# Splitting each 1 MB weight unit with one copy and one subtraction of 2048 columns

## The chip, the cores and the metric

The kernel runs on one core of a Trainium2 chip. The metric is the time of one execution in device microseconds (us); lower is better. One execution of the kernel before was also taken by the hardware profiler, and every row below is from that execution.

## The reference

Two transformer-like blocks, one after the other, on 256 tokens of width 2048, all in float32. Cut to the matrix products and what hangs between them:

```python
# first block
h = rms_norm(x, norm_mix_pre)
qa, ka, va, qn, kn, vn, gates = split(h @ w_in)
oa = rms_norm(diff_attention(rope(qa), rope(ka), va, lam), subln_w)
on = neighbourhood_attention(qn, kn, vn, na_rpb)
g_a, g_b = split(sigmoid(gates))
y = (g_a * (oa @ w_branch_a) + g_b * (on @ w_branch_b)) @ w_out
x = x + rms_norm(y, norm_mix_post)
u = square(relu(rms_norm(x, norm_mlp_pre) @ w_up))
x = x + rms_norm(u @ w_down, norm_mlp_post)
# second block
proj = rmsnorm(x, norm_w) @ w_in2          # mLSTM and HGRN2 inputs, gates ml_i, ml_f
y = concat(mlstm(...), hgrn2(...))
h = x + y @ w_out2
gate = sigmoid(rmsnorm(h, pe_norm_w) @ w_pg)
out = rmsnorm(h + gate * (p @ w_pe), final_norm_w)
```

The weights are float32 and each is used once, for 256 tokens.

## The kernel before, in words

**Numbers.** A float32 product is made of three products in the format fp32r: the weight is split into a high part `wh` (the weight rounded by a copy) and a low part `wl` (the weight less `wh`); the activation likewise into hi and lo. TensorE then adds hi·wh, hi·wl and lo·wh in PSUM.

**Weight units.** The weights come in units of 1 MB, a raw tile of 128 x 2048 float32 (8 KB in each partition; pool `raw`, three buffers), each by one DMA on SP's queue (`load_unit`). `split_w` splits a unit in two halves of 1024 columns: ScalarE (ACT) copies raw to `wh` (L100), VectorE (DVE) subtracts `wh` from raw to give `wl` (L101). The tiles of `wh` and `wl` are half a unit each, 4 KB in a partition, and the pool `wsplit` has four buffers of each, so two units' worth. A copy into a buffer waits until the last matmul that read the buffer's old half is done. There are 334 full units, so 668 copies and 668 subtractions; the first matrix, w_0, is split by lines of its own in the startup loop (L327, L328).

**Who uses a unit.** `panel` (L115 to L147) makes a 256 x 512 result from several units, 24 matmuls of 128x512 a unit (L128 hi·wh, L129 hi·wl, L130 lo·wh), for the two token tiles t=0 and t=1 in turn. For the last `lead` units it does all of t=0 first and then t=1, so that what follows for t=0 begins early; lead is 2 for the last panel of w_out, of w_down and of w_pg, and 1 elsewhere. `chunk_mm` (L149 to L173) makes a transposed 128-column result from one unit: 8 wide matmuls on `wh` (L156), 16 narrow ones on `wl` (L161), 8 wide. `chunk_pair` (L187, L192) does the first two units of w_up together, k-tile by k-tile, while their input is still being transposed. `embed` (L555 to L557) multiplies p by the two units of w_pe, between the end of a panel and the transposes of the residual.

**What sets the order.** Nothing is ordered by hand apart from a few priorities: a scheduler of the framework puts each engine's instructions into a list, and each engine runs its own list strictly in that order. An instruction that waits holds back everything behind it on its engine. Weight copies and subtractions stand in the same lists as all the other work of ACT and DVE.

**Places that the steps touch.** The q and k chunks with their rotary embedding (L358 to L361 after `halves`, L200 and L201), which also wait for a transfer of small columns, `cols`; the attention (L422 to L445); the post-norms after w_out and w_down (`yw` L607, sums L271 and L564, updates of the residual `res` L577, transposes L257, their splits L247 and L248, `embed`); the gate of the mLSTM (`log_f`, transposed sums L836, gate L837); the final panels of w_pg with their sigmoid (L979) and the closing norm (`finish`, L991 to L1006).

Of the kernel before, what the change touches and what calls it, by code (L numbers as in the profile page):

```python
# [9 lines left out]
F32 = mybir.dt.float32  # L10
F32R = mybir.dt.float32r
I8 = mybir.dt.int8
I32 = mybir.dt.int32
AF = mybir.ActivationFunctionType
ALU = mybir.AluOpType
AX = mybir.AxisListType

P = 128
# [39 lines left out]
def body(nc, tc, a, tap=lambda n, x: None):  # L58
    with ExitStack() as ctx:
        _body(ctx, nc, tc, a, tap)  # L60


def _body(ctx, nc, tc, a, tap):
    V, S, G, TE = nc.vector, nc.scalar, nc.gpsimd, nc.tensor

    def pool(name, bufs=1, psum=False, stack=ctx):
        kw = {"space": bass.MemoryType.PSUM} if psum else {}
        return stack.enter_context(tc.tile_pool(name=name, bufs=bufs, **kw))

    cpool = pool("const")  # L70
    rawp = pool("raw", 3)
    wp = pool("wsplit", 4)
    actp = pool("act", 16)
    mmp = pool("mm", 4, True)
    tpp = pool("tp", 2, True)
# [4 lines left out]
    def nm(s):  # L80
        uid[0] += 1
        return f"{s}_{uid[0]}"
# [10 lines left out]
    def act2():  # L93
        return actp.tile([P, 2, 2, T], F32R, tag="act", name=nm("act"))


    def split_w(r):
        wh = wp.tile([P, 1024], F32R, tag="wh", name=nm("wh"))
        wl = wp.tile([P, 1024], F32R, tag="wl", name=nm("wl"))
        S.activation(wh, r, AF.Copy)  # L100
        V.tensor_tensor(wl, r, wh.bitcast(F32), ALU.subtract)  # L101
        return wh, wl

    def load_unit(src):
        raw = rawp.tile([P, 2048], F32, tag="raw", name=nm("raw"))
        nc.sync.dma_start(raw, src)
        parts = []
        for h in range(2):
            parts.append(split_w(raw[:, h * 1024 : (h + 1) * 1024]))
        return parts  # L110

    pending = []

# [4 lines left out]
    def panel(src, acts, nunits, lead=1):  # L118


        ps = [ps_mm(), ps_mm()]
        nk = nunits * 4

        def step(t, kt, parts):
            k = kt % 4
            wh, wl = (w[:, (k % 2) * 512 : (k % 2 + 1) * 512] for w in parts[k // 2])
            h, l = acts.hi(kt, t), acts.lo(kt, t)
            TE.matmul(ps[t], h, wh, start=(kt == 0), stop=False)  # L128
            TE.matmul(ps[t], h, wl, start=False, stop=False)  # L129
            TE.matmul(ps[t], l, wh, start=False, stop=(kt == nk - 1))  # L130

        last = []
        for u in range(nunits):
            parts = load_unit(src[u])
            if u >= nunits - lead:
                last.append((u, parts))
                continue
            for kt in range(4 * u, 4 * u + 4):
                for t in range(2):
                    step(t, kt, parts)  # L140
            if u == 0:
                flush()
        for t in range(2):
            for u, parts in last:
                for kt in range(4 * u, 4 * u + 4):
                    step(t, kt, parts)
        return ps  # L147
# [23 lines left out]
    def chunk(src, acts):  # L171
        parts = load_unit(src)
        ps = ps_mm()  # L173
        chunk_mm(ps, parts, acts, 16)
        flush()
        return ps

    def chunk_pair(src_a, src_b, acts):

        parts = [load_unit(src_a), load_unit(src_b)]  # L180
        ps = [ps_mm(), ps_mm()]
        for kt in range(16):
            w = [[p[kt // 8][s][:, (kt % 8) * P : (kt % 8 + 1) * P] for s in range(2)] for p in parts]

            def wide():
                for i in range(2):
                    TE.matmul(ps[i], w[i][0], acts.both(kt), start=(kt == 0), stop=(kt == 15))  # L187

            if kt < 15:
                wide()  # L190
            for i in range(2):
                TE.matmul(ps[i][:, 0:T], w[i][1], acts.hi(kt), start=False, stop=False)  # L192
            if kt == 15:
                wide()
        return ps
# [90 lines left out]
    def later(tile_, src, after):  # L286

        G.tensor_copy(tile_[0:1, 0:1], after)
        nc.gpsimd.dma_start(tile_, src)
# [24 lines left out]
    for g in range(8):  # L314
        xn.tiles.append(act2())
        raw = raws[g // 2][:, g % 2 * 1024 : (g % 2 + 1) * 1024]
        wh = wp.tile([P, 1024], F32R, tag="wh", name=nm("wh"))
        wl = wp.tile([P, 1024], F32R, tag="wl", name=nm("wl"))
        n = 2 if g == 0 else 1
        for j in range(2):  # L320
            kt = 2 * g + j
            c, h, x = cols0[:, kt : kt + 1], xn.hi(kt), xts[g // 2][:, kt % 4, :]
            S.activation(h, x, AF.Copy, scale=c)
            V.scalar_tensor_tensor(xn.lo(kt), x, c, h.bitcast(F32), ALU.mult, ALU.subtract)
            if j < n:
                sl = slice(j * 1024 // n, (j + 1) * 1024 // n)
                S.activation(wh[:, sl], raw[:, sl], AF.Copy)  # L327
                V.tensor_tensor(wl[:, sl], raw[:, sl], wh[:, sl].bitcast(F32), ALU.subtract)  # L328

        def mm(j, c, part):  # L330
            kt = 2 * g + j
            sl = slice((4 * j + c) * P, (4 * j + c + 1) * P)
            if part == 0:
                TE.matmul(first[c], wh[:, sl], xn.both(kt), start=(kt == 0), stop=(kt == 15))
            else:
                TE.matmul(first[c][:, 0:T], wl[:, sl], xn.hi(kt), start=False, stop=False)

        if g < 7:
            for j in range(2):
                for part in range(2):  # L340
                    for c in range(4):
                        mm(j, c, part)
        else:
            for c in range(4):
                for j, part in ((0, 0), (0, 1), (1, 1), (1, 0)):
                    mm(j, c, part)
        if g == 1:
            there = xn.hi(2 * g)[0:1, 0:1].bitcast(F32)
            cstA = tA.tile([P, NCONST_A], F32, name="cstA")
            later(cstA, a["constsA"], there)  # L350
# [154 lines left out]
    for c in range(32):  # L505
        g = gates[c // 4][:, c % 4, :]
# [7 lines left out]
    for c in range(16):  # L514
        parts = load_unit(a["w_br"][c])
        ps = [ps_mm(), ps_mm()]
        for b, acts in enumerate((oa, on)):
            g = gates[4 * b + c // 4][:, c % 4, :]
# [91 lines left out]
    parts = load_unit(a["w_pe"][0])  # L610
# [38 lines left out]
    parts = load_unit(a["w_pe"][1])  # L649
# [476 lines left out]
```

## Time and profile before

| | us |
|---|---|
| three runs | 2010.0, 2006.1, 2008.21 |
| their median | 2008.21 |
| the profiled execution, whole | 2008.86 |
| its span in the profile | 2006.7 |
| PE (TensorE matmuls) busy | 1983.7, 99% |
| DVE busy, ACT busy | 1221.2 (61%), 1019.4 (51%) |
| POOL (GpSimd) busy | 156.5 (8%) |
| DMA, mean rate over the span | 185 GB/s |

The span is the time from the first to the last instruction of the profiled execution; the 2.2 us between it and the whole lie around it. PE is TensorE's matmuls, PEld its weight loads, which overlap them. The profile's granted clock is a share of TensorE's full speed; over the span its mean is 0.996. A row of a timeline gives start, duration, engine, line, operation, tiles and, in brackets, how long the engine had been idle before and what ended that. Matmul ends are modelled in such a profile, so the distance from one start to the next is the better measure of a matmul.

### The profile page before, as it was taken

What the parts mean: (1) busy time and instruction counts of PE and PEld (TensorE: products, weight loads), DVE (VectorE), ACT (ScalarE), POOL (GpSimd) and SP (SyncE); (2) the same over time, 40 slices, a digit from 0 to 9 for tenths busy, and PEclk for the clock granted to TensorE, in tenths of its full rate; (3) what the DMA queues carried; (4) which work ended last, traced back from release to release, by engine and by line L of the source; (5) the groups of instructions that cost most, each with busy time, mean ns of one, the idle gap of its engine ahead of it and who ended that gap; (6) DMA issues with size and microseconds to landing.
All of it is one profiled execution on the core that took longest, in us unless ns stands there. A gap on an engine that the chain in (4) does not pass through costs nothing. (4 is left out here: it accounts for less than half of the span.)

```text
span 2006.7 us, 25627 instructions
## 1 busy us (share of the span) xinstructions
PE 1983.7 (99%) x10192; PEld 1684.4 (84%) x10192; DVE 1221.2 (61%) x1574; ACT 1019.4 (51%) x1491; POOL 156.5 (8%) x190
## 2 busy tenths in 40 slices
PE   9999999999999999999999999999999999999997
PEld 7888888888888888888888888887788877888886
DVE  6756546555765765466556556656567864565565
ACT  6756446544554654455345434445543445444465
POOL 1400102111220000000000000010001110000011
PEclk9999999999999999999999999999999999999999
DMA  7753554455566455555555555555553344555553
GB/s 263 245 199 118 189 189 162 163 189 189 185 234 223 175 202 189 191 188 190 197 195 190 192 189 189 189 193 175 193 175 140 106 168 141 185 191 198 187 189 126
DMA packets 54375, 370.74 MB, mean 185 GB/s; under 512 B 6112, under 2 KB 6400, under 8 KB 10736
## 3 DMA queue, kind: packets, MB, share of 16 engines
q1 hardware_dynamic: 52208, 360.21, 51.0%
q0 software_dynamic: 1760, 8.38, 1.1%
q8 instruction: 80, 1.31, 0.3%
q10 hardware_dynamic: 288, 0.52, 0.1%
q14 instruction: 39, 0.32, 0.0%
HBM read 366.99 MB, written 2.10 MB: 184 GB/s over the span
## 5 line engine op out<-in xcount | busy, mean ns | idle before, releaser
L101 DVE TENSOR_TENSOR wl<-raw,wh 128x1024 fp32r<-128x1024 f32 x668 | 838.5, 1257 | 450.9 <-ACT wh L100 441.6
L100 ACT ACTIVATE wh<-raw 128x1024 fp32r<-128x1024 f32 x668 | 705.6, 1057 | 430.1 <-PE mm L130 365.1
L156 PE MATMUL mm<-act,wh 128*128 128x512 f32 x2592 | 634.5, 393 | 0.0
L156 PEld LDWEIGHTS mm<-act,wh 128*128 128x128 f32 x2592 | 473.4, 188 | 89.2
L128 PE MATMUL mm<-wh,act 128*128 128x512 f32 x1344 | 525.6, 391 | 0.8 <-ACT act L247 0.8
L129 PE MATMUL mm<-wl,act 128*128 128x512 f32 x1344 | 524.8, 390 | 0.4 <-DVE wl L101 0.4
L130 PE MATMUL mm<-wh,act 128*128 128x512 f32 x1344 | 524.4, 390 | 0.0
L161 PEld LDWEIGHTS mm<-act,wl 128*128 128x128 f32 x2592 | 335.8, 191 | 15.5 <-DVE wl L101 1.5
L161 PE MATMUL mm<-act,wl 128*128 128x256 f32 x2592 | 343.7, 283 | 1.1 <-DVE wl L101 1.1
L128 PEld LDWEIGHTS mm<-wh,act 128*128 128x128 f32 x1344 | 253.0, 188 | 53.6 <-ACT act L247 1.2
L129 PEld LDWEIGHTS mm<-wl,act 128*128 128x128 f32 x1344 | 253.0, 188 | 53.5 <-DVE wl L101 1.2
L130 PEld LDWEIGHTS mm<-wh,act 128*128 128x128 f32 x1344 | 252.9, 188 | 52.9 <-issue 0.6
L200 ACT ACTIVATE z<-mm 128x256 f32<-128x256 f32 x159 | 60.8, 383 | 280.4 <-PE mm L156 277.0
L201 DVE TENSOR_TENSOR zu<-mm,z 128x256 f32<-128x256 f32 x64 | 27.1, 425 | 110.5 <-ACT z L200 110.4
L648 POOL TENSOR_TENSOR yw<-yw,wrow 128x512 f32<-128x512 f32 x6 | 7.8, 1307 | 686.7 <-ACT junk L271 686.7
L201 DVE TENSOR_TENSOR g<-mm,z 128x256 f32<-128x256 f32 x48 | 20.2, 424 | 63.8 <-ACT z L200 63.8
L200 ACT ACTIVATE zl<-mm 128x256 f32<-128x256 f32 x24 | 9.1, 379 | 62.8 <-PE mm L156 62.8
L508 POOL TENSOR_TENSOR g<-g,r1row 128x256 f32<-128x256 f32 x32 | 23.7, 741 | 146.4 <-DVE g L201 146.4
L271 ACT ACTIVATE junk<-res 128x512 f32<-128x512 f32 (+1 forms) x40 | 21.7, 543 | 18.7 <-DVE res L964 11.6
L247 ACT ACTIVATE act<-tp,cols 128x256 fp32r<-128x256 f32 x56 | 24.7, 477 | 11.2 <-DVE act L248 8.5
L732 PEld LDWEIGHTS at<-g,g 128*128 128x128 f32 x224 | 26.4, 191 | 3.0 <-issue 2.5
L522 POOL TENSOR_TENSOR g<-g,zm 128x256 f32<-128x256 f32 x32 | 23.7, 742 | 65.8 <-DVE zm L201 65.8
(300 smaller groups left out, 1051.8 us busy)
## 6 DMA issues: line engine op xcount, KB each, us to landing
raw<-in_w_q SPq DMA_DIRECT2D x84, 1024.0 KB, 4.8
raw<-in_w_up SPq DMA_DIRECT2D x64, 1024.0 KB, 4.8
raw<-in_w_down SPq DMA_DIRECT2D x64, 1024.0 KB, 4.8
raw<-in_w_in SPq DMA_DIRECT2D x40, 1024.0 KB, 4.8
raw<-in_w_out SPq DMA_DIRECT2D x32, 1024.0 KB, 4.8
raw<-in_w_v SPq DMA_DIRECT2D x16, 1024.0 KB, 4.8
raw<-in_w_br SPq DMA_DIRECT2D x16, 1024.0 KB, 4.8
raw<-in_w_pg SPq DMA_DIRECT2D x16, 1024.0 KB, 4.8
```

The costliest lines, as they stand in the source:

```text
L100: S.activation(wh, r, AF.Copy)
L101: V.tensor_tensor(wl, r, wh.bitcast(F32), ALU.subtract)
L128: TE.matmul(ps[t], h, wh, start=(kt == 0), stop=False)
L129: TE.matmul(ps[t], h, wl, start=False, stop=False)
L130: TE.matmul(ps[t], l, wh, start=False, stop=(kt == nk - 1))
L156: TE.matmul(ps, w, acts.both(kt), start=(kt == 0), stop=(kt == nk - 1))
L161: TE.matmul(ps[:, 0:T], w, acts.hi(kt), start=False, stop=False)
L200: S.activation(lo, ps[:, T : 2 * T], AF.Copy)
L201: V.tensor_tensor(out, ps[:, 0:T], lo, ALU.add)
L247: last = S.activation(h, src[:, i, :], AF.Copy, scale=colscale(kt + i))
L508: G.tensor_tensor(g, g, r1row, ALU.mult)
L732: TE.matmul(ps[:, h, :], kk[:, h, b0 : b0 + P], q[:, h, b0 : b0 + P], start=True, stop=True)
```

## The change

A unit is split by one copy and one subtraction of 2048 columns. The tiles of `wh` and `wl` are whole units of 8 KB in a partition, with two buffers of each in place of four halves: the same bytes, and the same two units' worth. The users get views of the two halves, so the matmuls are the same. The startup loop keeps its instructions and shares one whole tile between two of its eight steps.

```diff
-    wp = pool("wsplit", 4)
+    wp = pool("wsplit", 2)
...
-    def split_w(r):
-        wh = wp.tile([P, 1024], F32R, tag="wh", name=nm("wh"))
-        wl = wp.tile([P, 1024], F32R, tag="wl", name=nm("wl"))
-        S.activation(wh, r, AF.Copy)
-        V.tensor_tensor(wl, r, wh.bitcast(F32), ALU.subtract)
-        return wh, wl
+    def split_tiles():
+        return (wp.tile([P, 2048], F32R, tag=tag, name=nm(tag)) for tag in ("wh", "wl"))
 
     def load_unit(src):
         raw = rawp.tile([P, 2048], F32, tag="raw", name=nm("raw"))
         nc.sync.dma_start(raw, src)
-        parts = []
-        for h in range(2):
-            parts.append(split_w(raw[:, h * 1024 : (h + 1) * 1024]))
-        return parts
+        wh, wl = split_tiles()
+        S.activation(wh, raw, AF.Copy)
+        V.tensor_tensor(wl, raw, wh.bitcast(F32), ALU.subtract)
+        return [(wh[:, h * 1024 : (h + 1) * 1024], wl[:, h * 1024 : (h + 1) * 1024]) for h in range(2)]
...
-        wh = wp.tile([P, 1024], F32R, tag="wh", name=nm("wh"))
-        wl = wp.tile([P, 1024], F32R, tag="wl", name=nm("wl"))
+        if g % 2 == 0:
+            wh2, wl2 = split_tiles()
+        wh, wl = (w[:, g % 2 * 1024 : (g % 2 + 1) * 1024] for w in (wh2, wl2))
```

ACT and DVE have 334 instructions fewer each, PE and SP as many as before. Because the scheduler weighs the durations of all instructions, the lists change in other places too. Line numbers of the changed kernel are two or three lower than those of the kernel before, and the two instructions of the split stand at L105 and L106. In the rows that follow, a name's first number is the tile's, so two rows with one name touch one tile.

DVE after w_out's last panel, before: `yw0` and `yw1` take the panel's results of t=0 and t=1, the L577 updates add them to the residual, and `wl_1090` and `wl_1092` are halves of w_pe's first unit.

```order
L607 TENSOR_TENSOR yw0_5358<-mm_1056_5801,wrow_5357 128x512
L564 TENSOR_REDUCE s_1080_5944<-s_983_5368 128x1
L101 TENSOR_TENSOR wl_1090_5964<-raw_1088_5961,wh_1089_5963 128x1024
L226 RECIPROCAL s_1082_5948<-s_1081_5946 128x1
L577 SCALAR_TENSOR_TENSOR res0_5349<-yw0_5358,s_1082_5948,res0_5349 128x512 x4
L101 TENSOR_TENSOR wl_1092_5968<-raw_1088_5961,wh_1091_5967 128x1024
L607 TENSOR_TENSOR yw1_5359<-mm_1057_5802,wrow_5357 128x512
```

The same place after the change (`wl_866` is w_pe's first unit, whole):

```order
L605 TENSOR_TENSOR yw0_4982<-mm_840_5377,wrow_4981 128x512
L562 TENSOR_REDUCE s_856_5504<-s_791_4992 128x1
L106 TENSOR_TENSOR wl_866_5524<-raw_864_5521,wh_865_5523 128x2048
L605 TENSOR_TENSOR yw1_4983<-mm_841_5378,wrow_4981 128x512
L562 TENSOR_REDUCE s_861_5515<-s_791_4992 128x1
L223 RECIPROCAL s_858_5508<-s_857_5506 128x1
L575 SCALAR_TENSOR_TENSOR res0_4973<-yw0_4982,s_858_5508,res0_4973 128x512 x3
```

The whole low part of w_pe's unit, and `yw1` too, now stand ahead of the first update of the residual; before, only half of the low part did.

ACT where the pair of w_up units ends, before: L271 are sums for the next norm, `z_1140` and `z_1143` take the pair's two results, and `wh_1147` and `wh_1154` are halves of weight units that follow the pair.

```order
L100 ACTIVATE wh_1147_6225<-raw_1144_6219 128x1024
L271 ACTIVATE junk_1131_6188,s_1125_6177<-res1_5350 128x512
L271 ACTIVATE junk_1132_6190,s_1125_6177<-res0_5349 128x512
L271 ACTIVATE junk_1133_6192,s_1125_6177<-res1_5350 128x512
L200 ACTIVATE z_1140_6205<-mm_1123_6111 128x256
L200 ACTIVATE z_1143_6213<-mm_1124_6112 128x256
L224 ACTIVATE s_1135_6196<-s_1134_6194,eps_78 128x2
L100 ACTIVATE wh_1154_6272<-raw_1153_6270 128x1024
```

The same place after the change (`wh_915` is the unit of the chunk that follows the pair):

```order
L268 ACTIVATE junk_903_5740,s_895_5725<-res1_4974 128x512
L221 ACTIVATE s_905_5744<-s_904_5742,eps_78 128x2
L197 ACTIVATE z_910_5753<-mm_893_5659 128x256
L197 ACTIVATE z_913_5761<-mm_894_5660 128x256
L105 ACTIVATE wh_915_5769<-raw_914_5767 128x2048
```

No copy of the next unit stands ahead of the pair's results any more; the first one stands behind both of them.

PE in the last panel of w_pg, after the change: `mm_2193` collects t=0 and `mm_2194` t=1; `wh_2202` and `wl_2203` are the last unit but one, `wh_2205` and `wl_2206` the last.

```order
L127 MATMUL mm_2193_14917<-wh_2202_14981,act_2095_14327 128x512
L125 MATMUL mm_2193_14917<-wh_2205_14987,act_2111_14439 128x512
L125 MATMUL mm_2194_14918<-wh_2202_14981,act_2093_14317 128x512
L126 MATMUL mm_2194_14918<-wl_2203_14982,act_2093_14317 128x512
L127 MATMUL mm_2194_14918<-wh_2202_14981,act_2093_14317 128x512
L125 MATMUL mm_2194_14918<-wh_2202_14981,act_2093_14317 128x512
L126 MATMUL mm_2194_14918<-wl_2203_14982,act_2093_14317 128x512
L127 MATMUL mm_2194_14918<-wh_2202_14981,act_2093_14317 128x512
L125 MATMUL mm_2194_14918<-wh_2202_14981,act_2095_14327 128x512
L126 MATMUL mm_2193_14917<-wl_2206_14988,act_2111_14439 128x512
```

Before, the matmul on the last unit's low part came directly behind the first one on its high part; now seven matmuls of t=1 lie between them. The same seven lie there in the last panels of w_out and of w_down.

DVE at the gate of the mLSTM, before (`gate` is made from the transposed sums `tp`, the two L837 instructions are for t=0 and t=1):

```order
L793 SCALAR_TENSOR_TENSOR g4_2317_13205<-g4_2353_13422,cols_77,g4_2317_13205 128x256 x3
L101 TENSOR_TENSOR wl_2415_13760<-raw_2413_13757,wh_2414_13759 128x1024
L837 SCALAR_TENSOR_TENSOR gate_13643<-tp_2407_13711,s_2075_11783,cols_77 128x8 x2
L841 TENSOR_SCALAR s_2393_13664<-gate_13643 128x8
L101 TENSOR_TENSOR wl_2417_13764<-raw_2413_13757,wh_2416_13763 128x1024
```

and after the change:

```order
L791 SCALAR_TENSOR_TENSOR g4_1785_12149<-g4_1813_12350,cols_77,g4_1785_12149 128x256 x3
L835 SCALAR_TENSOR_TENSOR gate_12555<-tp_1857_12619,s_1591_10823,cols_77 128x8 x2
L839 TENSOR_SCALAR s_1845_12576<-gate_12555 128x8
L106 TENSOR_TENSOR wl_1863_12664<-raw_1861_12661,wh_1862_12663 128x2048
```

The subtraction that stood ahead of the gate stands behind it.

## Rows read from the trace of the kernel before

**Rows 1.** The page: busy time of each engine, and the two costliest groups.

```profile
PE 1983.7 (99%) x10192; PEld 1684.4 (84%) x10192; DVE 1221.2 (61%) x1574; ACT 1019.4 (51%) x1491; POOL 156.5 (8%) x190
...
L101 DVE TENSOR_TENSOR wl<-raw,wh 128x1024 fp32r<-128x1024 f32 x668 | 838.5, 1257 | 450.9 <-ACT wh L100 441.6
L100 ACT ACTIVATE wh<-raw 128x1024 fp32r<-128x1024 f32 x668 | 705.6, 1057 | 430.1 <-PE mm L130 365.1
```

**Rows 2.** PE's waits over the span: total us, times, longest us.

```profile
PE tp L267 <- POOL A L718: 2.0, 1, 2.0
PE tp L836 <- DVE gate L837: 1.8, 1, 1.8
...
PE mm L161 <- DVE wl L101: 1.1, 1, 1.1
```

**Rows 3.** Waits of SP's queue, the longest sum, same columns.

```profile
SPq L106 <- DVE wl L101: 1327.8, 239, 17.0
```

**Rows 4.** Groups by shape, startup: busy us, mean ns, idle us before.

```profile
L328 DVE TENSOR_TENSOR wl<-raw,wh 128x1024 fp32r<-128x1024 f32 x7 | 8.6, 1225 | 1.7 <-ACT wh L327 1.7
...
L327 ACT ACTIVATE wh<-raw 128x1024 fp32r<-128x1024 f32 x7 | 7.4, 1060 | 1.3 <-DVE act L324 0.5 <-DMA raw<-in_w 0.4
L328 DVE TENSOR_TENSOR wl<-raw,wh 128x512 fp32r<-128x512 f32 x2 | 1.4, 692 | 0.9 <-ACT wh L327 0.9
L327 ACT ACTIVATE wh<-raw 128x512 fp32r<-128x512 f32 x2 | 1.2, 622 | 0.9 <-DMA raw<-in_w 0.9
```

**Rows 5.** Timeline of ACT in a steady panel of w_down.

```profile
830.21 1.06 ACT L100 ACTIVATE wh<-raw 128x1024 fp32r<-128x1024 f32 x1 [1.66 <-PE mm L130]
832.93 1.06 ACT L100 ACTIVATE wh<-raw 128x1024 fp32r<-128x1024 f32 x1 [1.66 <-PE mm L130]
```

**Rows 6.** Timeline of ACT, then of DVE, in the first q chunks.

```profile
30.78 1.05 ACT L100 ACTIVATE wh<-raw 128x1024 fp32r<-128x1024 f32 x1
...
40.73 0.16 DVE L390 TENSOR_TENSOR s<-cols 128x2 f32<-128x2 f32 x1 [3.11 <-DMA cols<-in_cols]
```

**Rows 7.** Groups of DVE by shape, the attention, 145 to 200 us.

```profile
L101 DVE TENSOR_TENSOR wl<-raw,wh 128x1024 fp32r<-128x1024 f32 x14 | 17.1, 1224 | 8.8 <-ACT wh L100 6.0 <-issue 2.7
```

**Rows 8.** Timeline after w_out's last panel, DVE, then ACT.

```profile
670.99 2.74 DVE L577 SCALAR_TENSOR_TENSOR res<-yw,s,res 128x512 f32<-128x512 f32 x4
...
674.78 0.68 DVE L607 TENSOR_TENSOR yw<-mm,wrow 128x512 f32<-128x512 f32 x1
...
691.76 1.04 ACT L100 ACTIVATE wh<-raw 128x1024 fp32r<-128x1024 f32 x1
...
694.93 0.66 ACT L200 ACTIVATE z<-mm 128x256 f32<-128x256 f32 x2
```

**Rows 9.** Timeline of DVE after w_down's last panel.

```profile
1388.29 0.75 DVE L577 SCALAR_TENSOR_TENSOR res<-yw,s,res 128x512 f32<-128x512 f32 x1
...
1393.47 2.73 DVE L577 SCALAR_TENSOR_TENSOR res<-yw,s,res 128x512 f32<-128x512 f32 x4
```

**Rows 10.** Timeline of DVE at the gate.

```profile
1627.53 1.46 DVE L101 TENSOR_TENSOR wl<-raw,wh 128x1024 fp32r<-128x1024 f32 x1 [1.71 <-ACT wh L100]
1628.91 0.21 DVE L837 SCALAR_TENSOR_TENSOR gate<-tp,s,cols 128x8 f32<-128x8 f32 x1
```

**Rows 11.** Stretches of 2 us behind it: PE busy (matmuls), granted clock, DMA share, GB/s.

```profile
1630.00:1632.00 2.00, 2.00 (x5) 0.50 0.00 0
1632.00:1634.00 2.00, 2.00 (x8) 0.75 0.79 197
```

**Rows 12.** Timeline of ACT in the last panel of w_pg.

```profile
1991.29 0.84 ACT L979 ACTIVATE g<-mm,s 128x256 f32<-128x256 f32 x2 [4.38 <-PE mm L130]
...
1996.42 0.20 ACT L994 ACTIVATE s<-s 128x1 f32<-128x1 f32 x1
1996.73 0.84 ACT L979 ACTIVATE g<-mm,s 128x256 f32<-128x256 f32 x2
```

**Rows 13.** Groups of DVE by shape, 570 to 586 us, where POOL works beside it.

```profile
L101 DVE TENSOR_TENSOR wl<-raw,wh 128x1024 fp32r<-128x1024 f32 x6 | 8.8, 1469 | 0.6 <-ACT wh L100 0.6
```

## The prediction

> **What bounds the kernel now.** I read the page first, then PE's waits, then the timelines at the places where PE waits or nearly does. The page says that PE is busy for 1983.7 of 2006.7 us, while DVE is busy for 61% and ACT for 51% of it [rows 1]. So the number of matmuls, which the change leaves alone, sets nearly all of the time. PE's waits on other engines are few and short; the largest that matter here are 2.0, 1.8 and 1.1 us [rows 2]. SP's queue waited 1327.8 us for low parts to be made [rows 3]: the loads are ready long before they are needed and are held back by buffers, not by the DMA. The splits wait too: the idle time ahead of L100 is ended by PE's matmuls, that ahead of L101 by ACT [rows 1]. In a steady panel ACT makes a half every 2.72 us, when PE has let go of a half buffer [rows 5]. Half a unit is 12 matmuls, so one matmul of 128x512 takes 2.72/12 = 0.227 us and a unit 5.44 us.
>
> So a change of the splits can only move the time where PE would wait for one, or where work in the same lists, for which PE waits, is held up or let through.
>
> **What a whole split costs.** The startup loop shows two sizes of each operation: ACT's copy takes 0.622 us for 512 columns and 1.060 for 1024, DVE's subtraction 0.692 and 1.225 [rows 4]. Along the same lines 2048 columns take 1.060 + 2 x 0.438 = 1.94 us and 1.225 + 2 x 0.533 = 2.29 us. Against two halves (2 x 1.057 and 2 x 1.257 us [rows 1]) that saves 0.17 and 0.22 us a unit, over 334 units 58 and 74 us of busy time. I cost this gain at nothing: it lies beside matmuls on engines that are a half and two fifths idle. Were there no such line and a whole split as dear as two halves, each would end up to 0.4 us later; this is a bound.
>
> [...]
>
> **What whole buffers cost in steady work: nothing.** Before, the copy of a half began when the matching half of an older unit was done. Now the copy for unit n+2 can't begin until the last matmul of unit n, and PE has only unit n+1 left to cover it. Copy and subtraction in a row take some 0.2 + 1.94 + 2.29 = 4.45 us, to the end of the low part. A panel needs it after 5.44 + 0.23 us. 1.2 us are left (before, over 5), and in a chunk more, since it reads the high part alone for its first 8 matmuls. So the MLP, the gates and most panels shouldn't move. The loads have room as well: each copy is delayed by less than a unit, with three raw buffers. Where other work stands among the splits, 1.2 us isn't enough. I followed the changed lists through each such place with the durations of the trace.
>
> **Start and q, k chunks: +3.5 us (0 to +7).** The first copy that had room at 30.78 us [rows 6] now waits until the startup's last matmuls, 1.6 us more, and lasts 0.9 longer. The rotary work behind it on ACT is 2.5 us late, and with it the POOL queue that issues the transfer of `cols`, for which DVE waited until 40.73 [rows 6]. A subtraction behind that on DVE then ends about 1.25 us too late; three chunks later in this stretch lose 0.8, 0.6 and 2.5, and the last 1.0, because a whole copy stands behind sums that wait for a load. That is +6.2, less the 1.1 of L161 that goes away [rows 2], +5. I take 3.5, since this chain rests on when a transfer is issued; if the copies slip past, it is 0.
>
> **Attention: +3 us (0 to +5).** Its 14 half subtractions of 1.22 us [rows 7] become 7 of 2.29, each in the middle of a softmax chain on DVE, so up to 7 x 1.07 = 7.5 later; chunk matmuls between cover more than half. The neighbourhood attention and HGRN2 have wider cover: 0, each within 2 us. In w_out's first panel ACT is held by a transfer; two halves in a row become whole: +1 (0 to 1.5).
>
> **After w_out: +5.2 us (+2 to +6.5).** The seven matmuls moved ahead let t=0's sums start 1.6 us later, and w_pe's first unit waits for a buffer until 669.9. Its copy ends at 671.8, its subtraction at 674.15, which is now ahead of `yw1` and of the first residual update. That update starts at 675.15 where it was 670.99 [rows 8]. PE has the embedding's 24 matmuls as cover, but waits about 0.95 for their own low part; two more whole subtractions stand among the splits of the transposes and cost 1.25, so the pair of w_up ends 2.2 us later. Then the move on ACT: before, half of a coming unit was copied at 691.76, ahead of the pair's results at 694.93 [rows 8]. Now the copy stands behind both results: 0.66 + 1.94 = 2.6 us in which PE has nothing, and 0.4 more for the low part. 2.2 + 3.0 = 5.2. The lower end is for a pair that ends on time and a copy that overlaps the last matmuls.
>
> **After w_down: +3.3 us (0 to +4).** Two whole subtractions stand ahead of the residual updates, which began at 1388.29 (t=0) and 1393.47 (t=1) [rows 9]. By the list t=1 begins about 4.5 us later and the panel behind it 3.45 later; a later wait, the 2.0 us at L267 [rows 2], stays about as long.
>
> **The gate: -3.5 us (-1.8 to -3.5).** Before, a subtraction waited until 1627.53 for its copy, took 1.46 us and stood ahead of the gate at 1628.91 [rows 10]; PE waited 1.8 us for it [rows 2]. In the new list the gate comes first. [...]
>
> **z panels and the end: +0.8 (-0.5 to +1) and +1.4 (+1.2 to +1.6).** The z panels trade a short wait for transposes against a late low part. In w_pg's last panel t=0 ends 7 x 0.227 = 1.6 us later, and all of ACT's chain for it, which ran from 1991.29 to 1996.62 [rows 12], moves with it. The sigmoid for t=1, which started at 1996.73 just when its matmuls were done, must wait for that chain until 1998.2. No work follows that could hide it. This is the surest term.
>
> **Sum.** 3.5 + 3 + 1 + 5.2 + 3.3 - 3.5 + 0.8 + 1.4 = +14.7 us on the profiled execution's 2008.86, 2023.6; that execution is 0.65 above the median of the runs, so against the median it is 2022.9. I say 2023.
>
> **Rivals.** *No change that can be measured* (a measurement of this kernel can tell 0.2%, 4 us, from no change). The early chunks and the attention are covered, the pair's copy overlaps, and what remains is the end, 2 to 3 us at the post-norms, and the gate: 1.4 + 2.5 + 2 - 3.5 = +2.4, about 2011. For it speaks that PE's lists have much other work to offer at all these places; against it that PE's list is fixed too.
>
> *Faster.* Fewer and cheaper pieces stand in the lists, and important work gets past them: the gate and its clock -3.5, L161 -1.1, part of L267 -1.5, with the end +1.4. That is -4.7, 2003.5 against the median, and less if the attention's chain gains too. It needs every whole copy outside the steady stages to be hidden under 5.44 us of matmuls; it turns where a copy stands behind an instruction that itself waits for PE, as the one behind the pair does.
>
> *Much slower.* The 1.2 us of room in a panel isn't there. Beside POOL's work the half subtraction took 1.469 us on average in place of 1.257 [rows 13]; a whole one would be 0.4 longer at that mean, and 1 us longer if each half met POOL as the slowest do. With an eviction or two between, some 15 to 30 units would each lose 0.5 to 1 us. [...] That gives 2033 to 2045. [...]
>
> [...]
>
> *The change doesn't do what it says*: a whole split is as dear as two halves. Then about ten of the waits above are 0.2 to 0.4 longer, +3: 2026. It lies within the forecast's range.
>
> **How the numbers follow.** Forecast, several places slower and steady work unmoved (2013 to 2033): 0.63, with the last rival in it. No change: 0.17 (2004.2 to 2012.2). Faster: 0.08. Much slower: 0.12. Slower by over 0.2% is the first and the last, 0.75. The range from 2008 to 2033 leaves out the faster case, about a quarter of the no-change case, and most of the much slower one, some 0.2 in all.
>
> **What would show it.** Whole copies near 1.94 and subtractions near 2.29 us, 334 of each; no waits on L105 or L106 in the MLP; PE idle about 2.6 us for a copy after the pair, near 697; a clock that stays at 1.00 behind the gate; t=1's last sigmoid over 1 us behind its last matmul. The forecast is wrong if PE's start-to-start gaps in the first 200 us are no longer than before, or if steady panels wait for low parts.

## The result and the profile after

The changed kernel took 2024.48 us (median of four runs, 2021.64 to 2025.48) against 2008.68 us before (four runs, 2006.1 to 2010.0): a ratio of 1.0076, 95% interval 1.0061 to 1.0091. It is slower by 0.8%; 2023.0 was forecast. The profiled execution took 2025.48 us with a span of 2023.5, 16.8 more than before. The page, its busy times and the two split groups:

```profile
PE 1986.9 (98%) x10192; PEld 1684.2 (83%) x10192; DVE 1159.1 (57%) x1240; ACT 949.7 (47%) x1157; POOL 176.0 (9%) x190
...
L106 DVE TENSOR_TENSOR wl<-raw,wh 128x2048 fp32r<-128x2048 f32 x334 | 768.9, 2303 | 565.1 <-ACT wh L105 564.3
L105 ACT ACTIVATE wh<-raw 128x2048 fp32r<-128x2048 f32 x334 | 638.2, 1911 | 412.7 <-PE mm L127 386.2
```

Against [rows 1] the copies take 67 us less and the subtractions 70 us less, near the 58 and 74 worked out from the startup's two sizes (a copy takes 1.91 us, a subtraction 2.30). None of it shortened the kernel. What was added stands in PE's waits (total us, times, longest us). Behind the startup those for `wh` or `wl` come to 16.4 us, where before they came to 1.5, 1.1 of it in [rows 2]. The longest sums:

```profile
PE mm L153 <- ACT wh L105: 6.2, 4, 2.3
PE mm L126 <- DVE wl L106: 3.9, 4, 1.8
PE mm L158 <- DVE wl L106: 2.8, 5, 1.0
PE mm L554 <- DVE wl L106: 2.2, 2, 1.2
PE tp L493 <- DVE e L491: 1.8, 4, 0.7
PE tp L254 <- DVE res L575: 1.7, 1, 1.7
```

PE runs the same 10192 matmuls in both kernels, so the start of its k-th instruction in one trace less that in the other tells how far behind the changed kernel is at each stage (the stretches left out, 368 to 597 and 620 to 666, moved by less than 0.05 us):

| stage (us in the trace before) | forecast | measured |
|---|---|---|
| start, q and k chunks, to 98 | +3.5 | +2.8 |
| v panels and attention, 98 to 294 | +3 | +0.1 |
| neighbourhood attention, to 368 | 0 | +1.4 |
| w_out's first panel, 597 to 620 | +1 | +3.7 |
| end of w_out, pair of w_up, 666 to 704 | +5.2 | +6.6 |
| MLP, 704 to 1372 | 0 | 0.0 |
| end of w_down, to 1418 | +3.3 | +0.9 |
| HGRN2, to 1597 | 0 | -0.6 |
| gate, to 1641 | -3.5 | -0.2 |
| z and other panels, to 1930 | +0.8 | +0.3 |
| w_pg and the end | +1.4 | +1.9 |
| sum | +14.7 | +16.8 (with rounding) |

The steady stages moved by nothing, in 668 us of MLP less than 0.05 us. At the end of w_out the lists did what was read from them. DVE's timeline there (start us, us, instruction, idle before):

```profile
679.93 2.29 DVE L106 TENSOR_TENSOR wl<-raw,wh 128x2048 fp32r<-128x2048 f32 x1 [1.61 <-ACT wh L105]
682.14 0.68 DVE L605 TENSOR_TENSOR yw<-mm,wrow 128x512 f32<-128x512 f32 x1
682.74 0.15 DVE L562 TENSOR_REDUCE s<-s 128x1 f32<-128x4 f32 x1
682.80 0.15 DVE L223 RECIPROCAL s<-s 128x1 f32<-128x1 f32 x1
682.99 2.08 DVE L575 SCALAR_TENSOR_TENSOR res<-yw,s,res 128x512 f32<-128x512 f32 x3
```

The first update of the residual starts at 682.99; less the 7.96 us that the kernel is behind here, that is 675.03, where 675.15 was forecast and 670.99 stood before [rows 8]. At the end of the pair, ACT:

```profile
705.30 0.66 ACT L197 ACTIVATE z<-mm 128x256 f32<-128x256 f32 x2 [0.96 <-PE mm L184]
705.84 1.91 ACT L105 ACTIVATE wh<-raw 128x2048 fp32r<-128x2048 f32 x1
```

and PE there, in stretches of 2 us (PE busy and matmuls, granted clock, DMA share, GB/s):

```profile
704.00:706.00 2.00, 1.49 (x9) 1.00 0.02 8
706.00:708.00 2.00, 0.20 (x1) 1.00 0.00 0
708.00:710.00 2.00, 2.00 (x8) 0.75 0.00 0
710.00:712.00 2.00, 2.00 (x10) 0.50 0.46 82
712.00:714.00 2.00, 2.00 (x14) 0.89 0.98 418
```

The copy comes behind both results, as forecast, and PE waits 2.3 us for it, where 2.6 were forecast. What the forecast's sum left out is the clock: it falls to 0.50 and costs about 1.7 us more before it is back at 1.00 (a quarter of one stretch, half of the next and a tenth of the third). The same happened at w_out's first panel. There ACT was held by the transfer of p until 612.88, the next copy came too late, and PE waited 1.8 us for a low part:

```profile
612.88 0.63 ACT L239 ACTIVATE pa<-pT 128x512 fp32r<-128x512 f32 x1 [5.47 <-DMA pT<-in_pT]
```

```profile
616.00:618.00 2.00, 0.84 (x3) 1.00 0.03 12
618.00:620.00 2.00, 1.01 (x4) 1.00 0.19 29
620.00:622.00 2.00, 2.00 (x7) 0.57 0.80 295
622.00:624.00 2.00, 2.00 (x7) 0.58 1.00 414
```

From 620.3 to 623.7 a matmul of 128x512 takes 0.43 us in place of 0.227: 8 matmuls, about 1.6 us.

Over the whole span, though, the lower clock cost no more than before. The trace before has three such falls ahead of its last matmul, near 12, 1630 [rows 11] and 1674 us, the changed kernel's three too, near 620, 709 and 1689. In stretches of 100 us a fall takes about 0.02 off the mean clock. Two rows of before, then two of the changed kernel:

```profile
0.00:100.00 100.00, 94.71 (x517) 0.98 0.71 254
1600.00:1700.00 100.00, 98.20 (x444) 0.97 0.45 154
...
0.00:100.00 100.00, 92.86 (x498) 1.00 0.69 245
1600.00:1700.00 100.00, 97.34 (x486) 0.98 0.42 148
```

At the gate, the wait and the lower clock of [rows 10, 11] are indeed gone, but just ahead of it three new waits for splits, 2.7 us together, appeared. Timelines of DVE, then of POOL:

```profile
1621.49 2.91 DVE L106 TENSOR_TENSOR wl<-raw,wh 128x2048 fp32r<-128x2048 f32 x1 [1.21 <-ACT wh L105]
...
1627.86 3.38 DVE L106 TENSOR_TENSOR wl<-raw,wh 128x2048 fp32r<-128x2048 f32 x1
```

```profile
1621.21 6.45 POOL L937 TENSOR_TENSOR g<-g,s 128x512 f32<-128x512 f32 x4
1627.62 1.47 POOL L796 TENSOR_TENSOR g<-g,z 128x512 f32<-128x512 f32 x1
```

The two subtractions shown, beside POOL's products, take 2.91 and 3.38 us instead of 2.29, and PE waits 0.6 and 1.0 us for their low parts; the third wait, 1.1 us and ahead of both, is for a copy that stood behind a table load of 1.28 us on ACT. That is 0.6 and 1.1 us added, though the second subtraction overlaps a product for only 1.2 us, as far as POOL's rough spans tell. It doesn't happen each time: the next subtraction, from 1633.41, overlaps a product for 1.4 us and takes 2.28, and there the product takes 2.51 us in place of 1.47. In the trace before, of the six halves of [rows 13], the three that overlap a product took 1.69 to 1.74 us and the three that don't 1.22. The trace shows the times, not what the two engines contend for.

The end, ACT in w_pg's last panel:

```profile
2008.31 0.84 ACT L977 ACTIVATE g<-mm,s 128x256 f32<-128x256 f32 x2 [5.20 <-PE mm L127]
...
2012.15 1.28 ACT L977 ACT_TABLE_LOAD   x1
2013.44 0.47 ACT L977 ACTIVATE g<-mm,s 128x256 f32<-128x256 f32 x1
```

The sigmoid for t=0 starts 17.02 us later than in [rows 12], though PE's matmuls start only 15.4 later here; the chain behind it lets t=1's start at 2013.44, 16.71 later than 1996.73.

### The profile page after: what moved, and what is told of

The parts are those of the page before. It is cut to its first block, busy times and chain, and to the rows that moved or that the text cites. A ratio compares the mean times of both kernels' runs of the same rounds, so it can differ in the third digit from the quotient of the medians.

```text
span 2023.5 us, 24821 instructions
## 1 busy us (share of the span) xinstructions
PE 1986.9 (98%) x10192; PEld 1684.2 (83%) x10192; DVE 1159.1 (57%) x1240; ACT 949.7 (47%) x1157; POOL 176.0 (9%) x190
## 4 chain that ended last, share of the span: by engine, by line
PE 88%; DVE 4%; ACT 3%; DMA 2%; POOL 2%; issue 1%; SPq 0%; DVEq 0%; ACTq 0%; POOLq 0%
PE mm L153 25%; PE mm L126 14%; PE mm L127 14%; PE mm L125 14%; PE mm L158 14%; DVE wl L106 2%; ACT wh L105 1%; PE at L730 1%; DMA pT<-in_pT 1%; POOL bias L471 1%; DMA bias<-in_rpb 1%; PE tp L254 1%; PE mm L332 0%; PE at L442 0%; PE at L420 0%
## 5 line engine op out<-in xcount | busy, mean ns | idle before, releaser
L106 DVE TENSOR_TENSOR wl<-raw,wh 128x2048 fp32r<-128x2048 f32 x334 | 768.9, 2303 | 565.1 <-ACT wh L105 564.3
L105 ACT ACTIVATE wh<-raw 128x2048 fp32r<-128x2048 f32 x334 | 638.2, 1911 | 412.7 <-PE mm L127 386.2
L646 POOL TENSOR_TENSOR yw<-yw,wrow 128x512 f32<-128x512 f32 x6 | 12.0, 1996 | 691.1 <-ACT junk L268 691.1
L985 POOL TENSOR_TENSOR res<-res,wfin 128x256 f32<-128x256 f32 x14 | 15.6, 1125 | 159.7 <-ACT junk L268 159.5
L268 ACT ACTIVATE junk<-res 128x512 f32<-128x512 f32 (+1 forms) x40 | 21.7, 541 | 16.4 <-DVE res L962 11.8
```

The lines of the kernel that those rows point to most:

```text
L105: S.activation(wh, raw, AF.Copy)
L106: V.tensor_tensor(wl, raw, wh.bitcast(F32), ALU.subtract)
```

## The experiments

The theory at first was that the time goes where a buffer is handed over only as a whole unit, in places where ACT or DVE has other work; its rival was the size of the operations, which stand whole in a list. Each run is compared with the kernel before on the same chip.

**Half operations in whole tiles.**

```diff
-        S.activation(wh, raw, AF.Copy)
-        V.tensor_tensor(wl, raw, wh.bitcast(F32), ALU.subtract)
+        for h in range(2):
+            c = slice(h * 1024, (h + 1) * 1024)
+            S.activation(wh[:, c], raw[:, c], AF.Copy)
+            V.tensor_tensor(wl[:, c], raw[:, c], wh[:, c].bitcast(F32), ALU.subtract)
```

> The changed kernel, but each unit split by two copies and two subtractions of 1024 columns, as before, into the same whole tiles (two buffers of 8 KB). Theory: what costs is that a buffer is handed over only when the whole old unit is done, so most of the loss stays, 2016 to 2022 us, with the wait for a copy after the pair of w_up and the wait at w_out's first panel still there (one to two us, since the first half is ready 1 us sooner). Rival, the size of the operations (a subtraction of 2.29 us that stands whole in DVE's list): about as the kernel before, 2008 to 2011 us.

It took 2011.8 us, a ratio of 1.0015 (1.0006 to 1.0025): just above the rival's range and far below the theory's. The hand-over was as late as in the changed kernel. In the MLP its ACT makes both halves in a row, once a unit:

```profile
851.57 2.01 ACT L107 ACTIVATE wh<-raw 128x1024 fp32r<-128x1024 f32 x2 [2.95 <-PE mm L129]
857.01 2.01 ACT L107 ACTIVATE wh<-raw 128x1024 fp32r<-128x1024 f32 x2 [3.43 <-PE mm L129]
```

So with the same buffers and the same hand-over, whole operations cost about 12 us more than halves. By the count along PE's list, from 666 to 704 us this kernel loses 1.6 us where the changed one loses 6.6. Its copy stands behind both of the pair's results too, but the first half is ready sooner: PE waits 1.5 us in place of 2.3, and a loss of 1.6 in all leaves no room for 1.7 more by the clock. At w_out's first panel it loses 4.9, more than the 3.7. The theory as first stated, that the late hand-over makes most of the loss, falls.

The count also shows where the size of the operations isn't the reason. At the start, where PE's list is the same, this kernel is 2.5 us behind at 98 us, nearly as much as the changed one (2.8). At the very end it loses nothing: the seven matmuls weren't moved in its list, so those 1.4 us of the changed kernel come from the order that the scheduler chose.

**Only one of the two whole.** The copy whole and the subtraction in halves:

```diff
         S.activation(wh, raw, AF.Copy)
-        V.tensor_tensor(wl, raw, wh.bitcast(F32), ALU.subtract)
+        for h in range(2):
+            c = slice(h * 1024, (h + 1) * 1024)
+            V.tensor_tensor(wl[:, c], raw[:, c], wh[:, c].bitcast(F32), ALU.subtract)
```

> The changed kernel with the copy whole (2048 columns) and the subtraction in two halves of 1024, whole tiles. Theory (hand-over of whole units): as the changed kernel within 4 us, 2020 to 2025 us. Rival (DVE's whole subtraction is what holds up other work): 2010 to 2015 us, with the stretch before the gate, where two subtractions took 2.9 and 3.4 us, no longer slower than before.

and the copy in halves, the subtraction whole:

```diff
-        S.activation(wh, raw, AF.Copy)
+        for h in range(2):
+            c = slice(h * 1024, (h + 1) * 1024)
+            S.activation(wh[:, c], raw[:, c], AF.Copy)
         V.tensor_tensor(wl, raw, wh.bitcast(F32), ALU.subtract)
```

> The changed kernel with two copies of 1024 and the subtraction whole (2048 columns), whole tiles. Theory (hand-over): 2018 to 2024 us. Rival (DVE's whole subtraction): as the changed kernel, 2022 to 2026 us, and 5 us or more above the kernel that has the copy whole and the subtraction in halves.

They took 2024.34 us (ratio 1.0079, 1.0062 to 1.0096) and 2039.73 us (1.0155, 1.014 to 1.017); the second lies above both of its expected ranges. So it isn't DVE's whole subtraction alone: with the copy whole nothing came back. A whole subtraction behind two copies is the worst of all. It can begin only when both copies are done, and at w_out's first panel other work stood between them in ACT's list: one half was copied at 605.19 us, then ACT waited for p's transfer. PE's longest sums of waits in that kernel, then ACT and DVE there:

```profile
PE mm L128 <- DVE wl L108: 8.8, 8, 5.1
PE mm L155 <- ACT wh L107: 6.1, 4, 3.7
...
611.95 0.63 ACT L241 ACTIVATE pa<-pT 128x512 fp32r<-128x512 f32 x1 [5.70 <-DMA pT<-in_pT]
612.48 1.04 ACT L107 ACTIVATE wh<-raw 128x1024 fp32r<-128x1024 f32 x1
...
613.55 2.29 DVE L108 TENSOR_TENSOR wl<-raw,wh 128x2048 fp32r<-128x2048 f32 x1 [0.25 <-ACT wh L107]
```

PE waited 5.1 us for that low part. This suggested a second theory: what counts is how long it takes from a buffer's release until the first piece of a unit can be read. With halves the first high part is there after 1.06 us and its low part after 2.3; with a whole copy after 1.9 and some 3.1; with both whole after 1.9 and 4.2. It fits the halves, but not these two kernels: by it the whole copy with halved subtractions should have beaten the changed kernel, and it came out level.

**p's split out of the way.** The first try put the statement later in the program:

```diff
-    split(pa, 0, pT)
...
+        if p == 1:
+            split(pa, 0, pT)
```

> The changed kernel with one statement moved: the split of p's transposed tile, which made ACT wait for a transfer until 612.9 us, stands after w_out's second panel. Theory: PE's 2.1 us wait for a low part at 617 us and the 3 to 4 us of half clock behind it both hang on ACT being held by that transfer, so about 3.7 us come back: 2020 to 2021.5 us, clock 1.00 from 616 to 626. Rival (the late copy only shows the room that whole buffers lack, and the next place takes it up): 2023 to 2025 us.

2026.22 us (1.0072 to 1.0102). It tests neither case: the scheduler left the instruction in its old place in ACT's list, and the 3.7 us at w_out's first panel were there again. The second try, also in the changed kernel, queues it behind named instructions:

```diff
+        if p == 1:
+            with tc.issue_after(last_s.ins), tc.issue_after(last_v.ins):
+                split(pa, 0, pT)
```

> The changed kernel with the split of p's transposed tile queued behind w_out's second panel's sums on ACT and behind its last product on DVE (the earlier try left it in its old place in the list). Theory: PE's wait of 2.1 us at w_out's first panel and the half clock behind it, 3.7 us together, hang on ACT being held by that transfer; they go, 2020 to 2021.5 us. Rival (the whole buffers lack room there anyway): 2023 us or more, with a wait for a low part left near 617 us.

2020.71 us (ratio 1.0063, 1.0049 to 1.0077). Between 597 and 620 us this kernel gained 0.7 us where it had lost 3.7, and the clock stayed up:

```profile
616.00:618.00 2.00, 2.00 (x11) 1.00 0.39 74
618.00:620.00 2.00, 2.00 (x11) 1.00 0.87 356
```

So that loss, the wait and the lower clock behind it, hung on ACT waiting for a transfer with the next unit's copy behind it. In the whole time the gain isn't clear of noise: the ratios 1.0063 and 1.0076 lie within each other's intervals. With half operations in whole tiles and the same edit:

> Half operations in whole tiles, with the split of p's tile queued behind w_out's second panel. Theory: the 4.9 us that this kernel lost at w_out's first panel come back, 2006.5 to 2008 us, 1 to 2.5 us below the kernel before. Rival: lost again at the next place, 2010 to 2012 us.

2005.36 us, ratio 0.9987 (0.9978 to 0.9996): 0.13% faster than the kernel before. That is a version that beats both, though the kernel before with the same edit wasn't run.

**The startup.** The changed kernel's profile was 2.35 us ahead at 27 us. Two runs asked whether that is of the change. The kernel with half operations again (its label names an edit that it doesn't have):

> The kernel with half operations in whole tiles, run a second time for another profile of the same program. Theory (the startup's gain of about 2.3 us against the profile of before is a matter of when transfers land): the times at the first weight matmuls differ from its first profile by 0.5 us or more. Rival (the shared tiles of the startup make it faster): the same gain again, 2.0 to 2.5 us at 27 us.

and the kernel before again:

> The kernel before, unchanged, for a second profile. All other profiles have the startup 1.5 to 2.8 us shorter at 27 us than the first profile of before. Theory (when transfers land, and the lower clock that follows a longer wait): this profile also has it 1 us or more shorter, and the 1.8 us wait at the gate with the half clock behind it is there again. Rival (the startup's sharing of tiles is a gain): the same startup as in the first profile within 0.5 us.

The second profile of before was 2.31 us ahead of its first at 27 us, and by 98 us level with it again (0.14). Its waits:

```profile
PE tp L267 <- POOL A L718: 2.0, 1, 2.0
PE mm L161 <- DVE wl L101: 1.9, 1, 1.9
PE tp L836 <- DVE gate L837: 1.8, 1, 1.8
```

The gain at the start is a matter of the execution, and is lost again in the next chunks; that is why the table takes the start and the q, k chunks together. The first profile waited 2.3 us for a copy at 11 us, and its clock was 0.92, 0.50 and 0.73 in the stretches of 2 us from 10 to 16 us; the second waited 0.8 there, its clock was 1.00 in these stretches, and it waited 1.9 us at L161, where the first waited 1.1. The half operations' second profile had 2.7 where the first had 2.24, so this run alone would have told nothing. It showed something else, below.

**The opposite direction.** The kernel before, with four pieces of 512 columns, each in its own tile:

```diff
-    wp = pool("wsplit", 4)
+    wp = pool("wsplit", 8)
...
-        wh = wp.tile([P, 1024], F32R, tag="wh", name=nm("wh"))
-        wl = wp.tile([P, 1024], F32R, tag="wl", name=nm("wl"))
+        wh = wp.tile([P, 512], F32R, tag="wh", name=nm("wh"))
+        wl = wp.tile([P, 512], F32R, tag="wl", name=nm("wl"))
...
-        for h in range(2):
-            parts.append(split_w(raw[:, h * 1024 : (h + 1) * 1024]))
+        for h in range(4):
+            parts.append(split_w(raw[:, h * 512 : (h + 1) * 512]))
```

> The kernel before with four splits of 512 columns a unit, each in tiles of its own (eight of 2 KB of each part): the opposite direction. Theory (what counts is how soon the first piece of a unit is ready and how long a piece holds up a list): no wait for a low part is left but the engines are busier by 0.4 us and 0.5 us a unit, 2004 to 2009 us. Rival (busy time of ACT and DVE counts, so fewer and larger operations are better): 2012 us or more.

1999.91 us, ratio 0.9958 (0.9944 to 0.9971): the fastest of all and below both expected ranges, though its splits cost more than those of before. Its groups by shape:

```profile
L101 DVE TENSOR_TENSOR wl<-raw,wh 128x512 fp32r<-128x512 f32 x1336 | 952.1, 727 | 529.1 <-ACT wh L100 505.3 <-PE mm L161 7.3 <-issue 4.2
L100 ACT ACTIVATE wh<-raw 128x512 fp32r<-128x512 f32 x1336 | 827.9, 629 | 630.7 <-PE mm L156 281.0 <-DVE wl L101 176.9 <-PE mm L130 114.9
```

That is 114 us more on DVE and 122 us more on ACT than in [rows 1], and the span is 8.1 us shorter (1998.6 us). From 666 to 704 us it gains 1.7 us. Some 5 of the 8.1 are the clock: the three falls of the kernel before, about 1.7 us each, are missing here. The one at the gate is there in its second profile too (0.68, 0.50 and 0.96 in the stretches of 2 us from 1630). The stretches in which before had 0.98 and 0.97:

```profile
0.00:100.00 100.00, 97.42 (x530) 1.00 0.74 263
1600.00:1700.00 100.00, 99.59 (x458) 1.00 0.47 169
```

**Small operations with the late hand-over**, four of 512 columns into whole tiles (the first diff with `range(4)` and 512):

> Four copies and four subtractions of 512 columns into whole tiles, two buffers of 8 KB: small operations with the late hand-over. Theory (both count: how soon the first piece is ready after a buffer is free, and when the buffer comes free): below half operations in whole tiles, 2006 to 2011 us, and 6 us or more above the quarters in tiles of their own. Rival (the hand-over hardly counts, only the size of an operation): 1999 to 2002 us.

2013.81 us, ratio 1.0026 (1.0015 to 1.0036): not below the half operations, as the theory had it, and 14 us above the quarters in tiles of their own. At w_out's first panel it waits longest:

```profile
PE mm L127 <- ACT wh L107: 2.6, 1, 2.6
```

**Smaller still**, tiles of 512 columns filled by two operations of 256 each:

> Tiles of 512 columns as in the quarters, each filled by two operations of 256 columns, eight copies and eight subtractions a unit. Theory: a 512-column piece is ready later (two copies of about 0.4 us for one of 0.63) and the engines are busier by about 0.7 us a unit on each, so nothing more is gained, 2000 to 2008 us. Rival (smaller is always better): 1996 to 1999 us.

2008.73 us, ratio 1.0003 (0.9993 to 1.0012), just above the theory's range. The page has DVE at 70% and ACT at 61% of its span. That the price of more instructions took the gain back is the likely reading: by the count it loses 1.7 us more than the quarters in the neighbourhood attention, at 294 to 368 us, and 4.1 more from 1600 to 1641. No run separated it from the order of the lists.

| operations of each part per unit | whole tiles, two buffers | tiles as large as a piece |
|---|---|---|
| 1 x 2048 | 2024.5 | |
| 2 x 1024 | 2011.8 | 2008.7 (before) |
| 4 x 512 | 2013.8 | 1999.9 |
| 8 x 256 | | 2008.7 (tiles of 512) |

Read across, the late hand-over costs 3 us with halves and 14 with quarters; read down, whole operations cost about 12 us more than halves with the same tiles. At the start the hand-over shows by itself: at 98 us every kernel with whole tiles is 2.3 to 4.3 us behind the first profile of before, whatever its operations, and the two with tiles of 512 columns are 2.9 and 2.3 ahead (before has lost 1.7 us to the clock by then; the quarters' mean clock there is 1.00). Both count, and neither alone explains the change. A third cause, that the scheduler orders the lists anew for each of these kernels, holds at least the 1.4 us at the end, and wasn't taken apart from them elsewhere: no run kept the lists fixed. Whole operations with a third buffer weren't tried either.

## Why the prediction was right, and where it was not

The direction, the size (+14.7 forecast, 15.8 between the medians) and the main reading were right: 99% of the time is matmuls, the saved busy time of 137 us is worth nothing, the steady stages don't move, and PE waits in the places where ACT's and DVE's lists carry other work. The range of 2008 to 2033 held the result. Four terms met their measure within 1.5 us: the start with the q and k chunks, the end of w_out with the pair, the z panels and the end. The first met it in part by luck. The first profile of before loses about 1.7 us to the lower clock by 98 us (the fall near 12), and the changed kernel's loses none (its mean clock there is 1.00), so its waits there cost some 4.5 us (2.8 and 1.7), near the +5 that was worked out and then taken as 3.5. The instructions followed there (the residual update, the copy behind the pair's results, the late sigmoid) stand in the rows above where they were expected.

The rest is right in sum because errors cancelled, which is luck.

- **Attention, +3, measured +0.1.** The step that failed is that chunk matmuls cover only "more than half" of the seven longer subtractions. They covered all of it: no wait for a split stands between 145 and 200 us. The neighbourhood attention, put at 0, lost 1.4 to waits for its exponentials.
- **w_out's first panel, +1, measured +3.7.** The blocked ACT was seen, but not that PE would wait 1.8 us for the low part and then run at the lower clock. The run that took the block away gained 4.4 us there over the changed kernel.
- **End of w_down, +3.3, measured +0.9.** The panel's start was 3.0 us later, near the 3.45 forecast, but the wait at L267 that was to stay "about as long" went: 2.2 us came back there.
- **The gate, -3.5, measured -0.2.** The gate's own wait and its clock went, as forecast, and gave back 3.5 us: 1.8 of wait and 1.7 of clock. No row adds up the 1.7; the trace before shows a clock of 0.90, 0.50 and 0.75 in the stretches of 2 us from 1628, which costs 0.2 + 1.0 + 0.5 = 1.7. The step left out the stretch just ahead, where two subtractions took 2.91 and 3.38 us beside POOL's products and a copy stood behind a table load of 1.28 us; 3.3 us were lost there.
- **The lower clock.** The sum counts a fall only behind the gate; the much slower case's 2033 to 2045 also counts 1.7 us for each new wait of 2 us and more, which no run shows as a rule. The lower clock came in two places of the forecast's own list, behind waits of 2.3 and 1.8 us, for some 3.3 us together, and in the trace before it didn't come behind the 2.0 us at L267 (1.00 in each stretch of 2 us from 1414 to 1422). The sum didn't suffer, because both traces have three falls: those of before, of which the forecast counted only the gate's, went, and three others came.

Of the rivals, the much slower case named what was measured before the gate (subtractions of 2.91 and 3.38 us beside POOL's products), but the steady panels, in which no wait appeared, kept their room. What the faster case counted on did come: the gate's 3.5 us, the 1.1 of L161 and 2.2 at L267; the new waits for splits outweighed it. The quarters speak against its reason, fewer and cheaper pieces: they have twice the pieces of before and are 0.4% faster.

## What to carry to other kernels

When one engine is 99% busy and others prepare its operands, choose the size of a preparing step by what the busy engine waits for, not by the step's cost per element: here halving the instructions cost 0.8%, doubling them gained 0.4%, much of it by the clock, and doubling again took that back. Keep the buffer as fine as the operation: quarters in whole tiles were no faster than halves in whole tiles, and 14 us slower than quarters in tiles of their own. And look for instructions that wait for a transfer with operand preparation behind them in the same list: moving one such instruction was worth 4.4 us at its place, and some 6 us of the whole time in the kernel with halves. Expect a new order of the lists with each such edit, and read it before the run.

## What was not expected of the hardware

In these traces the granted clock made some short waits dearer by 1.6 to 1.7 us, and others not. After 2.3 us without a matmul at the pair it fell to 0.50, and after PE had been busy for 0.84 and 1.01 us of two successive stretches of 2 us at w_out it fell to 0.57; near 84 us, in these two stretches and in the two behind them, it stayed at 1.00:

```profile
84.00:86.00 2.00, 0.64 (x3) 1.00 0.00 0
86.00:88.00 2.00, 1.69 (x7) 1.00 0.00 0
```

And in the trace before it fell near 1674 us, where the profile shows PE busy throughout and no wait of PE: from 1670 us on short products, of 4x256 and 128x128, stood among the matmuls:

```profile
1672.00:1674.00 2.00, 2.00 (x8) 0.99 0.00 0
1674.00:1676.00 2.00, 2.00 (x6) 0.50 0.47 98
```

POOL's same 190 instructions were busy for 176.0 us against 156.5 [rows 1]; the products of the rotary embedding (L357, before L359) took 24.4 of it against 15.1. What lengthens them was not shown; with the copy in halves and the subtraction whole POOL was busy for 163.7 us.

The same program can also differ from one execution to the next: the half operations in whole tiles had a clock of 1.00 from 1660 to 1700 us in their first profile and of 0.94 and 0.89 in their second, which was 3.2 us behind the first by 1930 us. The stretches in the second:

```profile
1660.00:1680.00 20.00, 20.00 (x81) 0.94 0.45 159
1680.00:1700.00 20.00, 20.00 (x83) 0.89 0.16 54
```
